# RMSNorm factors of a hybrid decoder layer: column sums turned to rows, or a product of ones with Ln, Exp and one Newton step

## Chip, core and metric

One NeuronCore of a Trainium2 chip runs the whole kernel. The metric is device microseconds of one execution, as the median of three runs. TensorE (PE) multiplies matrices, VectorE (DVE), ScalarE (ACT) and GpSimd (POOL) work element by element, SyncE (SP) issues most of the transfers.

## What is computed

One layer for 512 prompt positions and 8 single decode steps, 520 columns in all, D_MODEL 1024. Four RMSNorms stand in it: ahead of the mixer, on the 256 memory tokens, ahead of the FFN, and at the end.

```python
def rmsnorm(x, g):
    y = xf * lax.rsqrt(jnp.mean(xf * xf, axis=-1, keepdims=True) + EPS)
    return y * g

h = rmsnorm(x, norm_mix_g)
q, k, v, u, xq, gates = split_cols(h @ w_in)
# A: sliding-window attention, B: S5 state space model, C: attention over the memory tokens
mk, mv = split(rmsnorm(mem, norm_mem_g) @ w_mem_kv)
merged = sig(gA) * P_A(A) + sig(gB) * B + sig(gC) * P_C(C)
x = x + merged @ w_out
h = rmsnorm(x, norm_ffn_g)
x = x + W_down(gelu(causal_dwconv3(h @ W_gate)) * (h @ W_up))
y = rmsnorm(x, norm_final_g)
```

## The kernel before

**Layout.** Activations are kept transposed: a block of 128 features on the partitions, 520 columns (two halves of 260) along the free axis, eight such blocks for D_MODEL. All f32 values are split in a high part in fp32r and the rest, and one block product is three matmuls (`mm3`). A weight unit is 128 x 1024: SP loads it into one of two `wraw` buffers, ACT copies the high part (`whi`), DVE subtracts the low part (`wlo`), three buffers of each (`w_split`, `load`, `begin`, `ahead`). `begin(i)` asks for the loads of i+1 and i+2, `ahead(i)` for the splits of i+1 and i+2 and the load of i+3. Products go to two PSUM tiles (`mm`, `out_tile`), smaller ones to four (`SD`). Each engine works its instructions off in the order in which the program writes them.

**The norm's factor is applied late.** The products are made with x times the gain alone (`split_norm`: high part on ACT, low part on DVE). The factor rstd differs by column only, so it is multiplied in when a product is emptied from PSUM. `rstd` has 520 columns, the same on all partitions. For the mixer and the FFN, `acc` and `acc2` hold the squares summed over the eight blocks, and the sum over the partitions is still to be made.

**How rstd was made.** `rstd_cols` multiplies pieces of 88 columns of the sums, as weights, with one column of ones, so that each piece's sums stand on 88 partitions: six products for 520 columns, three for the memory's 256. DVE makes 1/sqrt on these few numbers: a bit trick and three Newton steps, twelve small operations, then a diagonal matrix of them. `rstd_rows` multiplies ones with the diagonal pieces, which puts each number on all partitions again, and ACT copies the rows out.

```python
dcol = rstd_cols([acc], (0, 1), NH)     # mixer: after the first block of q0 (Q_COL)
ahead(iq)
rstd_rows(dcol, rstd)                   # mixer: eleven blocks later (Q_ROW)
ps = product(i, range(8), blk(yh, yl), kouter=True, mid=norm2)                            # FFN: fg0
pu = product(i, range(8), blk(yh, yl), kouter=True, mid=lambda: rstd_rows(dcol, rstd))    # FFN: fu0
```

**Order around the mixer.** k and v are multiplied side by side as x arrives, into both `mm` tiles; then q0 into two `SD` tiles. `evac_kv` empties k and v on DVE with rstd, two multiplications each, then q0. The next unit, q1, writes k's tile. `x_norm` then makes the fully normalised x (DVE, ACT, DVE per block) beside q1 to q3, for the u, xq and gate units that follow.

**A planner orders the rest.** Softmax of the window attention, the memory's norm (`mem_prep`), S5 and memory attention are generators ("lanes"). `pump` runs their next steps between block products, when a clock model of all engines (`Clock`) says that the step's operands are ready; `drain` runs a lane to its end. So an instruction's place in the streams depends on the modelled times of all before it. `mem_prep` ends with the two norm steps, and `mem_kv` drains it ahead of the first memory product.

**Order around the FFN.** The out units write x1, its squares go to `acc2`. fg0 and fu0 run with all eight blocks in turn, both halves; the norm's two parts stand in the middle of the one and the other. Then DVE empties fg0 with rstd, and a lane does the convolution (`conv`: POOL, ACT, DVE twice, POOL, Gelu on ACT) and a second multiplication by rstd, after which DVE empties fu0. The next pairs fg1, fu1 use the same two tiles. Beside them a lane builds the combinations of normalised x for a Strassen product (`y_lane`).

**Activation tables.** Exp, Tanh, Gelu and Ln need a table on ACT; the loads are instructions on its queue. The kernel asks for one by name near the end, for the final norm, which uses Ln, Exp and a Newton step (`Piece.ln_exp`, `Piece.newton`).

Of the kernel before, what the change touches and what calls it, by code (L numbers as in the profile page):

```python
# [15 lines left out]
P = 128  # L16
# [270 lines left out]
N_RAW = 2  # L287
N_T2 = 11
Q_COL = (0, 0)
Q_ROW = (1, 2)  # L290
N_SWA = 2
N_MEM = 3

# [1 line left out]
def body(ctx, tc, I, O):  # L295
# [20 lines left out]
    def B(dt=F32):  # L316
        live["B"] += 1
        assert live["B"] <= 8, "no slot left"
        return big.tile([P, KB * NT], dt, name="B", tag="B")
# [12 lines left out]
    def free(*ts):  # L332
        for t in ts:
            clk.pinned.discard(t.name)
# [9 lines left out]
    def T2(n=NT, dt=F32):  # L344
        t = make(tmp, [P, 528], dt, "T2", N_T2)
        return t[:, :n]

    def TN(n):
        t = clk.tile(tny.tile([P, 8], F32, name="TN", tag="TN"), "TN", 16)
        return t[:, :n]  # L350

    def SD():
        return make(psd, [P, 512], F32, "SD", 4)
# [137 lines left out]
    def product(i, js, xs, kouter=False, mid=None):  # L491

        ps = out_tile()
        n = len(js)
        ev[0] = EV_FF if clk.late else EV if n == 8 else EVH
        if kouter:
            for k, j in enumerate(js):
                wh, wl = hl(i, j)
                for h in range(H):
                    xh, xl = xs(k, h)  # L500
                    mm3(ps[:, h, :NH], wh, wl, xh, xl, k == 0, k == n - 1)
                if k == n // 2:
                    ahead(i)
                    if mid:
                        mid()
            pump()
        else:
            for h in range(H):
                for k, j in enumerate(js):
                    wh, wl = hl(i, j)  # L510
                    xh, xl = xs(k, h)
                    mm3(ps[:, h, :NH], wh, wl, xh, xl, k == 0, k == n - 1)
                    if k % GRAIN == GRAIN - 1 and (h == 0 or k < n - 1):
                        if h == 0 and k >= 3:
                            ahead(i)
                        pump(0.325 * ((1 - h) * n + n - 1 - k))
        return ps[:, :, :NH]
# [10 lines left out]
    eps = con.tile([P, 1], F32, name="eps")  # L528
    dve.memset(eps, EPS)
    warm = con.tile([P, 1], F32, name="warm")  # L530
    act.activation(warm, ones[:, 0:1], AF.Exp)
    xraw = B()

    def x_load(k, n):
# [29 lines left out]

    RB = 88

    def starts(n):
        return (0, (n - RB) // 2, n - RB)

    def rstd_cols(parts, halves, n):  # L570

        ps = SD()
        nb = 3 * len(halves)
        for a, h in enumerate(halves):
            for b, s in enumerate(starts(n)):
                c = 3 * a + b
                for e, x in enumerate(parts):
                    pe.matmul(ps[:RB, c:c + 1], x[:, h * n + s:h * n + s + RB], ones[:, 0:1], start=e == 0,
                              stop=e == len(parts) - 1)
        v, y, t = TN(nb)[:RB], TN(nb)[:RB], TN(nb)[:RB]  # L580
        it = tny.tile([P, 16], I32, name="it", tag="it", bufs=2)[:RB, :nb]
        dve.tensor_scalar(v, ps[:RB, :nb], 1.0 / DM, EPS, op0=OP.mult, op1=OP.add)
        dve.tensor_scalar(it, v.bitcast(I32), 1, None, op0=OP.logical_shift_right)
        dve.tensor_scalar(it, it, -1.0, 1597463007.0, op0=OP.mult, op1=OP.add)
        free(ps)
        y0 = it.bitcast(F32)
        for n_ in range(3):
            dve.tensor_tensor(t, y0, y0, op=OP.mult)
            dve.scalar_tensor_tensor(t, t, -0.5, v, op0=OP.mult, op1=OP.mult)
            dve.scalar_tensor_tensor(y, t, 1.5, y0, op0=OP.add, op1=OP.mult)  # L590
            y0 = y
        d = T2(528)[:RB, :nb * RB].rearrange("p (b c) -> p b c", b=nb)
        dve.tensor_tensor(d, ident[:RB, None, :RB].to_broadcast([RB, nb, RB]),
                          y[:, :, None].to_broadcast([RB, nb, RB]), op=OP.mult)
        return d

    def rstd_row(d, a, n, ps):

        for b, s in enumerate(starts(n)):
            pe.matmul(ps[:, s:s + RB], ones[:RB, :], d[:, 3 * a + b, :], start=True, stop=True)  # L600

    def rstd_rows(d, out, n=NH, halves=(0, 1)):
        for a, h in enumerate(halves):
            ps = SD()
            rstd_row(d, a, n, ps)
            act.activation(out[:, h * n:(h + 1) * n], ps[:, :n], AF.Copy)
            free(ps)


    sv = con.tile([P, 528], F32, name="sv")  # L610
# [156 lines left out]
    sp.dma_start(mraw, I["memT"])  # L767
    iq = begin("q")
    psq = [SD(), SD()]
    dcol = None  # L770
    for h in range(H):
        for k in range(KB):
            wh, wl = hl(iq, k)
            xh, xl = xg(k, h)
            mm3(psq[h][:, :NH], wh, wl, xh, xl, k == 0, k == KB - 1)
            if (h, k) == Q_COL:
                dcol = rstd_cols([acc], (0, 1), NH)
                ahead(iq)
            if (h, k) == Q_ROW:
                rstd_rows(dcol, rstd)  # L780

    ud = drm.tile([8, 4, P, 64], F32, name="ud")
    us = drm.tile([4, P, 8], F32, name="us")
# [20 lines left out]
    def mem_prep():  # L804
        macc = T2(256)
        for k in range(KB):
            split_norm(mraw, C_GMEM, mgh, mgl, k, 256)
            sq = macc if k == 0 else T2(256)
            act.activation(sq, mraw[:, k * 256:(k + 1) * 256], AF.Square)
            if k:  # L810
                dve.tensor_tensor(macc, macc, sq, op=OP.add)
                free(sq)
            yield 1 if k == KB - 1 else "dve", 1
        d = rstd_cols([macc], (0,), 256)
        free(macc)
        yield
        rstd_rows(d, mrstd, 256, (0,))
        free(d)
        yield

    qB = B()
# [776 lines left out]
    def blk(hi, lo):  # L1598
        def f(k, h):
            o = k * NT + h * NH  # L1600
            return hi[:, o:o + NH], lo[:, o:o + NH]
        return f

    B_done(3)

    yh, yl = B(F32R), B(F32R)
    acc2 = T2()
    for m in range(8):
        i = begin("out")
# [63 lines left out]
    cpv = cpre.rearrange("p o (h b) -> p o h b", h=H)  # L1673

    def norm2():
        nonlocal dcol
        dcol = rstd_cols([acc2], (0, 1), NH)


    def conv(ob, a, c):  # L1680
# [352 lines left out]
    for ob in range(6):  # L2033
        if ob == 4:
            for name in ("A11", "S", "A12", "A22"):
                strassens[0].load(name, -1)
            cu.append(svt[:, 0:512])
            for _ in range(3):
                cu.append(hold(make(tmp, [P, 528], F32, "T2", N_T2))[:, 0:512])
            for j in range(4):  # L2040
                dparts[j][0].load(dparts[j][1])
        i = begin("fg")
        if ob == 0:

            ps = product(i, range(8), blk(yh, yl), kouter=True, mid=norm2)
            i = begin("fu")
            pu = product(i, range(8), blk(yh, yl), kouter=True, mid=lambda: rstd_rows(dcol, rstd))
            y_build = add(y_lane(), need=0, tiles=3)
            y_build.eng = "dve"
        else:  # L2050
            ps = product(i, range(8), blk(yh, yl))
        a = hold(make(tmp, [P, 528], F32, "T2", N_T2))[:, :524]
        av = wide(a)
        c = hold(T2())
        dve.tensor_tensor(av[:, :, 2:], ps, rs2, op=OP.mult)

        def first_lane(ob=ob, av=av, c=c):
            yield from conv(ob, av, c)
            yield "dve"
            dve.tensor_tensor(c, c, rstd, op=OP.mult)  # L2060

        def second_lane(ob=ob, c=c, a=a):
            act.activation(hid(ob, 0), c, AF.Copy)
            yield "dve"
            dve.tensor_tensor(hid(ob, 1), c, hid(ob, 0).bitcast(F32), op=OP.subtract)
            free(a, c)

        l = add(first_lane(), first=True, need=0)
        l.eng = "act"
        if ob:  # L2070
            i = begin("fu")
            if ob == 5:
                for s in range(D_HI):
                    cut(s, "hi")
                    if s < D:
                        cut(s, "lo")
            pu = product(i, range(8), blk(yh, yl))
        drain([l])
        dve.tensor_tensor(hv(c), pu, hv(c), op=OP.mult)
        hid_lanes[-ob] = add(second_lane(), first=True, need=0)  # L2080
        hid_lanes[-ob].eng = "act"
        while later:
            later.pop(0)[1]()

    ln = tny.tile([P, 1], F32, name="ln", tag="ln", bufs=1)
    drain([hid_lanes[-q] for q in range(6)])
    B_done(2)
    hb[1], hb[2] = B(F32R), B(F32R)
# [21 lines left out]
    class Piece:  # L2110
# [28 lines left out]
        def newton(self):  # L2139
            t = T2(self.n)  # L2140
            dve.tensor_tensor(t, self.y, self.y, op=OP.mult)
            dve.scalar_tensor_tensor(t, t, -0.5, self.v, op0=OP.mult, op1=OP.mult)
            dve.scalar_tensor_tensor(self.y, t, 1.5, self.y, op0=OP.add, op1=OP.mult)
# [195 lines left out]
```

## Time and profile before

| | |
|---|---|
| median of 3 runs | 869.74 us (869.24 to 870.06) |
| profiled execution | 870.38 us, span 868.6 us |
| PE busy | 851.2 us (98%) |
| DVE busy | 599.8 us (69%) |
| ACT busy | 409.0 us (47%) |
| POOL busy | 135.7 us (16%) |
| mean granted clock of TensorE | 0.997 |

The span is from the first to the last instruction. The profiled execution is 1.78 us longer than its span. Busy times of PE count each matmul to its modelled end, so that neighbours overlap; what a matmul costs in a running stream is read from the distance of two starts. The source column reads L259 for nearly all, a helper's line, so that stages are told by tile names and times.

### The profile page before, as it was taken

What the parts mean: (1) busy time and instruction counts of PE and PEld (TensorE: products, weight loads), DVE (VectorE), ACT (ScalarE), POOL (GpSimd) and SP (SyncE); (2) the same over time, 40 slices, a digit from 0 to 9 for tenths busy, and PEclk for the clock granted to TensorE, in tenths of its full rate; (3) what the DMA queues carried; (4) which work ended last, traced back from release to release, by engine and by line L of the source; (5) the groups of instructions that cost most, each with busy time, mean ns of one, the idle gap of its engine ahead of it and who ended that gap; (6) DMA issues with size and microseconds to landing.
All of it is one profiled execution on the core that took longest, in us unless ns stands there. A gap on an engine that the chain in (4) does not pass through costs nothing.

```text
span 868.6 us, 17715 instructions
## 1 busy us (share of the span) xinstructions
PE 851.2 (98%) x7067; PEld 823.0 (95%) x7067; DVE 599.8 (69%) x1101; ACT 409.0 (47%) x800; POOL 135.7 (16%) x370
## 2 busy tenths in 40 slices
PE   8999999999999999999999999999999999999996
PEld 8998899999789899989999999999999999999995
DVE  6786787985447698213765568787777877777756
ACT  7366565544434322223334434444645545464555
POOL 7888030000000000000000010111112110110100
PEclk9999999999999999999999999999999999999998
DMA  7534482253714523624333323557565655653222
GB/s 264 178 78 122 125 196 80 74 154 116 150 49 146 170 74 97 148 69 184 106 101 97 98 73 100 144 155 185 152 160 151 165 130 153 161 150 83 71 74 98
DMA packets 54737, 110.41 MB, mean 127 GB/s; under 512 B 13968, under 2 KB 25664, under 8 KB 54384
## 3 DMA queue, kind: packets, MB, share of 16 engines
q1 hardware_dynamic: 50816, 97.40, 38.0%
q0 software_dynamic: 3408, 11.27, 6.8%
q8 instruction: 55, 0.90, 0.4%
q10 hardware_dynamic: 432, 0.63, 0.2%
q14 instruction: 26, 0.21, 0.1%
HBM read 104.05 MB, written 6.26 MB: 127 GB/s over the span
## 4 chain that ended last, share of the span: by engine, by line
PE 74%; DVE 11%; issue 9%; ACT 3%; DMA 2%; SPq 0%; POOL 0%; DVEq 0%; ACTq 0%; POOLq 0%
PE mm L259 55%; PE SD L259 19%; DVE T L259 5%; DVE B L259 3%; DVE wlo L259 2%; DMA wraw<-in_w 2%; ACT T L259 1%; ACT whi L259 1%; ACT B L259 1%; DVE TN L259 1%; SPq L259 0%; POOL T L259 0%; DVE M L259 0%; DVEq L2334 0%; DVE it L259 0%
## 5 line engine op out<-in xcount | busy, mean ns | idle before, releaser
L259 PE MATMUL mm<-B,whi 128*128 128x260 f32 (+1 forms) x3632 | 666.5, 284 | 3.5 <-DVE B L259 1.4
L259 PEld LDWEIGHTS mm<-B,whi 128*128 128x128 f32 x3632 | 560.3, 188 | 11.9 <-issue 5.0
L259 PE MATMUL mm<-B,wlo 128*128 128x260 f32 (+1 forms) x1816 | 512.8, 282 | 1.9 <-DVE wlo L259 1.9
L259 PEld LDWEIGHTS mm<-B,wlo 128*128 128x128 f32 x1816 | 342.2, 188 | 2.8 <-DVE wlo L259 2.8
L259 DVE TENSOR_TENSOR wlo<-wraw,whi 128x1024 fp32r<-128x1024 f32 (+1 forms) x149 | 152.4, 1029 | 89.2 <-ACT whi L259 86.2
L259 ACT ACTIVATE whi<-wraw 128x1024 fp32r<-128x1024 f32 (+1 forms) x149 | 132.5, 897 | 73.0 <-PE mm L259 32.6
L259 PE MATMUL SD<-B,whi 128*128 128x260 f32 x464 | 85.9, 282 | 0.0
L259 PEld LDWEIGHTS SD<-B,whi 128*128 128x128 f32 x464 | 71.6, 188 | 0.1
L259 ACT ACTIVATE T<-mm 128x260 f32<-128x260 f32 (+3 forms) x76 | 32.5, 449 | 78.1 <-PE mm L259 78.0
L259 PE MATMUL SD<-B,wlo 128*128 128x260 f32 x232 | 65.6, 283 | 0.0
L259 ACT ACTIVATE B<-T 128x520 fp32r<-128x520 f32 (+2 forms) x48 | 29.7, 618 | 55.5 <-DVE T L259 55.4
L259 ACT ACTIVATE whi<-M 128x512 fp32r<-128x512 f32 x64 | 39.1, 624 | 26.3 <-DVE M L259 19.4
L259 DVE TENSOR_TENSOR wlo<-M,whi 128x512 fp32r<-128x512 f32 x64 | 42.8, 686 | 11.9 <-ACT whi L259 11.8
L259 DVE TENSOR_TENSOR B<-B 128x256 f32<-128x256 f32 (+11 forms) x78 | 36.3, 474 | 15.9 <-ACT B L259 14.4
L259 PEld LDWEIGHTS SD<-B,wlo 128*128 128x128 f32 x232 | 43.6, 188 | 0.0
L259 DVE TENSOR_TENSOR B<-mm,B 128x520 f32<-128x520 f32 (+2 forms) x36 | 22.4, 622 | 27.4 <-PE mm L259 26.8
L259 ACT ACTIVATE B<-SD 128x256 fp32r<-128x256 f32 (+5 forms) x44 | 17.9, 429 | 44.3 <-PE SD L259 44.3
L259 DVE TENSOR_TENSOR B<-SD,B 128x256 fp32r<-128x256 f32 (+6 forms) x43 | 16.5, 396 | 30.3 <-PE SD L259 22.7
L259 PE MATMUL SD<-B 128*64 128x72 f32 (+9 forms) x412 | 37.3, 282 | 0.0
L259 DVE SCALAR_TENSOR_TENSOR T<-T,sm,T 128x512 f32<-128x512 f32 x44 | 33.1, 753 | 2.7 <-ACT T L259 2.2
L259 DVE TENSOR_TENSOR B<-T,B 128x520 fp32r<-128x520 f32 (+2 forms) x50 | 31.2, 637 | 3.7 <-ACT B L259 3.4
L259 PEld LDWEIGHTS SD<-B 128*64 128x64 f32 (+4 forms) x412 | 25.6, 146 | 8.3 <-issue 4.0
(161 smaller groups left out, 801.8 us busy)
## 6 DMA issues: line engine op xcount, KB each, us to landing
wraw<-in_w SPq DMA_DIRECT2D x96, 512.0 KB, 3.6
M<-in_w SPq DMA_DIRECT2D x48, 256.0 KB, 3.6
wraw<-in_w SPq DMA_DIRECT2D x36, 256.0 KB, 3.3
T<-in_w SPq DMA_DIRECT2D x36, 192.0 KB, 4.4
M<-in_w POOLq DMA_DIRECT2D x8, 512.0 KB, 6.6
wraw<-in_w POOLq DMA_DIRECT2D x8, 512.0 KB, 6.3
sv<-in_w SPq DMA_DIRECT2D x12, 192.0 KB, 5.5
B<-in_xT SPq DMA_DIRECT2D x1, 2080.0 KB
```

The lines of the kernel that those rows point to most:

```text
L259: return g(*a, **k)
```

## The change

Both helpers go. `rstd_sums` multiplies a matrix of ones with the sums, which gives the total on all partitions at once, and ACT makes exp(-0.5 ln(v)) from it; ACT also writes v, the mean square plus EPS. `newton` does one Newton step on full width on DVE. In the mixer all of it stands after q0's first block, with q1's split between Exp and the copies of v (`then`). In the memory's lane it is two steps. In the FFN it stands in the middle of fg0, and nothing in fu0. A table set with Ln and Exp is asked for at the start, in place of the set that Exp brought, and again ahead of the out units.

```diff
+    ln = con.tile([P, 1], F32, name="ln")
+    nc.scalar.preload_act_table_set("natural_log_exp_and_others")
-    act.activation(warm, ones[:, 0:1], AF.Exp)
+    act.activation(warm, ones[:, 0:1], AF.Ln)
...
-    def rstd_cols(parts, halves, n):
...
-    def rstd_rows(d, out, n=NH, halves=(0, 1)):
...
+    def rstd_sums(part, out, n=NH, halves=(0, 1), then=None):
+        pr = [SD() for _ in halves]
+        for p, h in zip(pr, halves):
+            pe.matmul(p[:, :n], ones, part[:, h * n:(h + 1) * n], start=True, stop=True)
+        for p, h in zip(pr, halves):
+            act.activation(out[:, h * n:(h + 1) * n], p[:, :n], AF.Ln, bias=eps, scale=1.0 / DM)
+        o = out[:, 0:len(halves) * n]
+        act.activation(o, o, AF.Exp, scale=-0.5)
+        if then:
+            then()
+        v = T2(len(halves) * n)
+        for p, h in zip(pr, halves):
+            act.activation(v[:, h * n:(h + 1) * n], p[:, :n], AF.Identity, bias=eps, scale=1.0 / DM)
+            free(p)
+        return v, o
+
+    def newton(v, o):
+        t = T2(o.shape[1])
+        dve.tensor_tensor(t, o, o, op=OP.mult)
+        dve.scalar_tensor_tensor(t, t, -0.5, v, op0=OP.mult, op1=OP.mult)
+        dve.scalar_tensor_tensor(o, t, 1.5, o, op0=OP.add, op1=OP.mult)
+        free(t, v)
...
             if (h, k) == Q_COL:
-                dcol = rstd_cols([acc], (0, 1), NH)
+                newton(*rstd_sums(acc, rstd, then=lambda: w_split(iq + 1)))
                 ahead(iq)
-            if (h, k) == Q_ROW:
-                rstd_rows(dcol, rstd)
...
-        d = rstd_cols([macc], (0,), 256)
+        v, o = rstd_sums(macc, mrstd, 256, (0,))
         free(macc)
-        yield
-        rstd_rows(d, mrstd, 256, (0,))
-        free(d)
+        yield "dve", 1
+        newton(v, o)
         yield
...
     yh, yl = B(F32R), B(F32R)
+    nc.scalar.preload_act_table_set("natural_log_exp_and_others")
+    act.activation(ln, ones[:, 0:1], AF.Ln)
     acc2 = T2()
...
     def norm2():
-        nonlocal dcol
-        dcol = rstd_cols([acc2], (0, 1), NH)
+        newton(*rstd_sums(acc2, rstd))
...
-            pu = product(i, range(8), blk(yh, yl), kouter=True, mid=lambda: rstd_rows(dcol, rstd))
+            pu = product(i, range(8), blk(yh, yl), kouter=True)
```

## Rows read from the trace of the kernel before

**Rows 1.** Page, part 1: busy us (share of the span) and instructions by engine

```profile
PE 851.2 (98%) x7067; PEld 823.0 (95%) x7067; DVE 599.8 (69%) x1101; ACT 409.0 (47%) x800; POOL 135.7 (16%) x370
```

**Rows 2.** Table by stretches: start:end and length, busy by engine, clock, DMA

```profile
core 0: us, PE busy (x) PEld busy (x) DVE busy (x) ACT busy (x) POOL busy (x), PEclk, DMA share, GB/s
45.00:160.00 115.00, 113.64 (x946) 104.25 (x945) 90.49 (x260) 73.08 (x204) 45.95 (x139) 1.00 0.45 118
520.00:582.00 62.00, 60.06 (x493) 59.09 (x491) 50.04 (x79) 28.05 (x45) 7.72 (x25) 1.00 0.48 132
```

**Rows 3.** Timeline, TensorE around q0: start us, length us, operation, out<-in, xcount

```profile
20.61 1.03 PE L259 MATMUL SD<-ones,T 128*88 128x1 f32 x12
...
21.50 0.48 PE L259 MATMUL SD<-B,whi 128*128 128x260 f32 x2
...
25.18 1.47 PE L259 MATMUL SD<-T,ones 88*128 88x88 f32 x12
...
26.44 0.48 PE L259 MATMUL SD<-B,whi 128*128 128x260 f32 x2
...
28.21 0.28 PE L259 MATMUL SD<-B,wlo 128*128 128x260 f32 x1
...
28.32 0.40 PE L259 MATMUL mm<-B,whi 128*128 128x260 f32 x2
```

**Rows 4.** Timeline, final norm: TensorE, ScalarE and VectorE

```profile
850.43 1.04 PE L259 MATMUL SD<-T,ones 128*128 128x260 f32 x4
...
851.12 0.59 PE L259 MATMUL SD<-B,whi 128*128 128x260 f32 x2
...
851.51 0.48 ACT L259 ACTIVATE T<-SD,eps 128x260 f32<-128x260 f32 x1 [1.42 <-PE SD L259]
...
852.02 0.42 ACT L259 ACTIVATE T<-T 128x260 f32<-128x260 f32 x1
...
853.01 0.89 DVE L259 SCALAR_TENSOR_TENSOR T<-T,T 128x260 f32<-128x260 f32 x2
```

**Rows 5.** Timeline, ScalarE and VectorE around q0; idle before, and releaser, in brackets

```profile
24.31 1.06 ACT L259 ACTIVATE whi<-wraw 128x1024 fp32r<-128x1024 f32 x1 [3.62 <-PE SD L259]
...
24.72 2.35 DVE L259 TENSOR_TENSOR wlo<-wraw,whi 128x1024 fp32r<-128x1024 f32 x2
...
27.11 1.43 DVE L259 TENSOR_TENSOR B<-mm,rstd 128x512 f32<-128x512 f32 x4
...
29.25 0.75 DVE L259 SCALAR_TENSOR_TENSOR T<-B,sm,rstd 128x520 f32<-128x520 f32 x1
```

**Rows 6.** Timeline, TensorE and VectorE around the FFN's norm

```profile
499.44 1.03 PE L259 MATMUL SD<-ones,T 128*88 128x1 f32 x12
...
506.15 1.47 PE L259 MATMUL SD<-T,ones 88*128 88x88 f32 x12
...
515.47 0.48 PE L259 MATMUL mm<-B,whi 128*128 128x260 f32 x2
...
508.07 0.70 DVE L259 TENSOR_TENSOR T<-mm,rstd 128x520 f32<-128x520 f32 x1 [3.02 <-ACT rstd L259]
...
514.63 0.70 DVE L259 TENSOR_TENSOR T<-mm,T 128x520 f32<-128x520 f32 x1
```

**Rows 7.** Timeline, TensorE around the memory's norm

```profile
68.98 0.56 PE L259 MATMUL SD<-ones,T 128*88 128x1 f32 x6
...
69.40 0.49 PE L259 MATMUL mm<-B,whi 128*128 128x260 f32 x2
...
75.13 0.87 PE L259 MATMUL SD<-T,ones 88*128 88x88 f32 x6 [1.17 <-DVE TN L259]
...
75.84 0.60 PE L259 MATMUL SD<-cs,T 128*128 128x128 f32 x4
```

**Rows 8.** Timeline, ScalarE: a first gate, the first FFN scaling, a table load

```profile
158.18 0.60 ACT L259 ACTIVATE B<-mm 128x520 f32<-128x520 f32 x1 [1.43 <-PE mm L259]
...
456.68 0.73 ACT L259 ACTIVATE B<-B,sm 128x520 fp32r<-128x520 f32 x1 [2.62 <-DVE B L259]
...
833.12 1.28 ACT L2102 ACT_TABLE_LOAD   x1
...
834.42 0.20 ACT L259 ACTIVATE ln<-ones 128x1 f32<-128x1 f32 x1
```

More of the change, by code (lines that the diff above doesn't have):

```diff
@@ L289 @@
 Q_COL = (0, 0)
-Q_ROW = (1, 2)
 N_SWA = 2
@@ L565, in body @@
     RB = 88
-    def starts(n):
-        return (0, (n - RB) // 2, n - RB)
-    def rstd_cols(parts, halves, n):
[L572 to L595, printed above, removed]
@@ L597, in rstd_row @@
-    def rstd_row(d, a, n, ps):
-        for b, s in enumerate(starts(n)):
-            pe.matmul(ps[:, s:s + RB], ones[:RB, :], d[:, 3 * a + b, :], start=True, stop=True)
-    def rstd_rows(d, out, n=NH, halves=(0, 1)):
[L603 to L607, printed above, removed]
+    def rstd_sums(part, out, n=NH, halves=(0, 1), then=None):
[13 more added lines that the diff above has]
+        return v, o
@@ L769, in body @@
     psq = [SD(), SD()]
-    dcol = None
     for h in range(H):
@@ L2083, in body @@
             later.pop(0)[1]()
-    ln = tny.tile([P, 1], F32, name="ln", tag="ln", bufs=1)
     drain([hid_lanes[-q] for q in range(6)])
```

## The prediction

> **What bounds the kernel now.** I read the busy shares of the page first, to see which engine has no room: TensorE is busy 98% of the span [rows 1], so the end moves only by work that TensorE no longer does, or by stretches in which it stands. Next the table by stretches, to see where it stands: 1.36 us between 45 and 160 us, and 1.94 us between 520 and 582 us [rows 2]. Then the timeline of single engines around the three places that the change touches: TensorE for the price of the old and new products, VectorE (DVE) and ScalarE (ACT) for who delivers the norm's factor, and whether TensorE is there first. The granted clock is 1.00 in both stretches [rows 2], so durations can be added as they stand.
>
> **Mixer, TensorE's work.** In the running stream a product of 260 columns follows the last by 0.11 to 0.12 us [rows 3]. The first old group starts at 20.61 and the stream goes on at 21.50: 0.89 us. The second starts at 25.18 and the stream goes on at 26.44: 1.26 us. Removed are 2.15 us. The new product, ones by 260 columns in f32, is already in the kernel at its end: two of them hold the stream from 850.43 to 851.12, so 0.69 us [rows 4]. The mixer needs two: 2.15 - 0.69 = 1.46 us saved. The square sums are ready where the old columns start, as the old group starts without a wait [rows 3], and the new products stand at the same place.
>
> **Mixer, the new wait.** The first q product after q0 writes the bank that k's product holds, and that is emptied by two DVE multiplications with rstd. Before, DVE did them from 27.11 (two of the four in that row, half of 1.43 us), free at about 27.85; TensorE came at 28.32 [rows 3, 5]. After, TensorE comes at 28.32 - 1.46 = 26.86. DVE's chain: the first new product is done some 0.74 us after 20.61 (the final norm's two are read 1.08 us after their start, and one is 0.35 less [rows 4]), so Ln starts at 21.35. Two Ln, 0.48 each and overlapping by 0.1: 22.2. Exp on 520 columns: 0.64, between the 0.42 for 260 and the 1.06 for 1024 [rows 4, 5]: 22.9. Now `then` puts q1's split in front of the rest: its high part on ACT, 1.06, ends at 23.9, and its low part stands on DVE ahead of the Newton step, half of 2.35 [rows 5]: 25.05. Newton, three dependent operations on 520 columns: 0.70 [rows 6], 0.75 twice [rows 5], with 0.05 between them as dependent ones don't overlap (0.89 for two of 260 [rows 4]): 27.3. `ahead` then puts q2's low part in front of the evacuation, another 1.17: 28.45; its weights were split at 24.31 before [rows 5] and stand on ACT behind the two Identity, so they are in time. Two multiplications: 29.2. TensorE restarts at 29.25, 0.93 us later than before: the 1.46 us are spent and a wait of 2.4 us comes. Behind the waiting product stand all of q1 to q3 and the u products. Bounds: +0.5 if each of eight steps overlaps by 0.05 more, +1.6 if the DVE chain, which is 28.45 - 27.11 = 1.34 late, also reaches the last normalised blocks of x before u0. I take +0.93, as TensorE is late by as much itself.
>
> **Memory.** Removed: 68.98 to 69.40, 0.42 us, and 75.13 to 75.84, 0.71 us [rows 7]; added one product of 256 columns, half of 0.69. Saved: 0.78 us. The second old group also stood 1.17 us for the DVE chain [rows 7]. After the change nothing of this norm follows on TensorE; three DVE operations on 256 columns remain, some 1.35 us (0.89 for two, and a third), and are wanted only when the first memory product is emptied, some 2.7 us later. Next on TensorE are transposes of an earlier softmax step and a product whose weights were split two units ahead. Gone are 0.78 + 1.17 = 1.95 us; bounds 0.78 (another late step takes the place) and 1.95.
>
> **FFN.** The same two groups, 1.03 and 1.47 [rows 6], go and two products come: 1.46 us. Before, the rows stood in the middle of fu0, and DVE idled 3.02 us up to 508.07 to empty fg0. After, sums at 499.44 give Exp at 501.7 by the chain above and Newton at 504.1 behind fg1's split; fu1's split (fg0 ends near 502.3, then 1.06 + 1.17) puts the first multiplication at 505.2, 2.9 us earlier. TensorE then needs fu0's bank for fu1 at 515.47 - 1.46 = 514.0. It is freed by the multiplication that started 6.56 us after 508.07 and lasts 0.70 [rows 6]; with the table load of Gelu, 1.28 [rows 8], that is 505.2 + 6.56 + 1.28 + 0.70 = 513.7. Just no wait, with 0.3 us of cover: if the cover is gone, it costs up to 0.5 us. Bounds for the stage: -1.0, and -3.4 if the 2.9 us that DVE gains also close the 1.94 us of [rows 2].
>
> **Table loads.** A load lasts 1.28 us [rows 8]. The one at the start is there before, with another set. The one ahead of the out products lies in ACT's idle time there (2.62 us ahead of the first scaling [rows 8]): nothing. If Tanh is not in the set with Ln, which no row shows, the first gate brings one more; ACT idles 1.43 us ahead of that Tanh [rows 8], so it is hidden too, and would cost up to 1.28 us of ACT in a stretch where TensorE is fed two products ahead. Gelu's is counted above.
>
> [rows 8] show a load that ends at 834.40 and the next operation at 834.42: no pause behind it. The Trainium skill, ScalarE: Activation LUTs, section What ACT_TABLE_LOAD costs, gives a switch about 2.66 us, a load of about 1283 ns and a drain of about 1380 ns. The 1283 ns agree, the drain isn't seen here. By that rule of the Trainium skill Gelu would come 1.38 us later and the sum would be some 1.3 us higher.
>
> **Sum.** +0.93 - 1.95 - 1.46 = -2.48 us. The profiled execution took 870.38 (span 868.6 and 1.78 around it), so 867.9; it lies 0.64 above the median of 869.74, which gives 867.26, say 867.3, 0.28% less. A measurement of this kernel can tell about 0.2%, 1.74 us: faster means below 868.0.
>
> **The rivals.**
> *More is freed.* DVE is done 2.9 us earlier at FFN's start, and the gaps of 520 to 582 are waits for DVE. For it: DVE is busy 50.0 of 62 us there [rows 2]. Against: DVE's order is fixed by the planner, not by who is ready. 867.3 - 1.94 = 865.3.
> *Only part stays.* Another late step takes the place of the memory norm's 1.17, and 0.3 of the mixer's DVE delay reaches u0: 867.3 + 1.5 = 868.8, no difference. For it: this stretch is fed by softmax steps on DVE and ACT, and the planner, whose clock now sees other durations, orders them anew.
> *DVE's backlog is handed on.* The evacuation is 1.34 late; if x's normalised blocks, the memory product and the last attention block are each handed to TensorE 1.34 late, with TensorE there in time, the sum is 0.93 - 0.78 - 1.46 + 4.0 = +2.7: 872.4. It decides from the third such hand-over on; one only cancels the gain. For it: DVE is busy 90.5 of 115 us between 45 and 160 [rows 2]. Against: TensorE itself is 0.93 late, which leaves 0.4 of each.
> *A pause behind the load.* If ACT stands behind Gelu's load as long again, 1.28 us, fu0's bank is late by 1.0: 868.3. [rows 8] speak against it at the one place where an operation follows at once. It is the drain of the Trainium skill's page named above.
>
> **How the numbers follow.** Forecast 0.50, more freed 0.15, only part 0.24, backlog 0.09, pause 0.02. The forecast's own bounds (+0.5 to +1.3 in the mixer, FFN -1.0 to -2.0) put a fifth of it above 868.0, and a fifth of "only part" falls below. Faster: 0.40 + 0.15 + 0.05 = 0.60. Slower: 0.09. Within 0.2%: 0.31. The range of 865.0 to 869.8 holds the forecast, "more freed", "only part" and the pause with some 0.3 to 1 us around each; the backlog and the tails, under 0.2, lie outside.
>
> **What would show it.** TensorE waits about 2.4 us for DVE near 27 us and restarts near 29.25. No wait of TensorE remains ahead of the first memory product near 75. Two more products of ones stand near 499.5 with no rows behind, and DVE empties fg0 near 505, not 508 (less the shift). Loads: one ahead of the out products, one ahead of the first fold's Gelu. I am wrong if TensorE's busy time falls by less than 3.5 us (the work alone is 1.46 + 0.78 + 1.46 = 3.7), or if the stretch from 30 to 240 us has more gaps than before.

## The result, and the profile after

| | before | after |
|---|---|---|
| median | 869.74 us | 879.10 us (876.03 to 882.13, 6 runs) |
| ratio | | 1.0108, 95% interval 1.0090 to 1.0125 |
| profiled execution, span | 870.38, 868.6 | 880.5, 878.7 |
| mean granted clock of TensorE | 0.997 | 0.989 |

The changed kernel is 9.4 us slower; forecast were 2.4 us less. The page, part 1, of the changed kernel:

```profile
PE 854.1 (97%) x7017; PEld 824.5 (94%) x7017; DVE 595.9 (68%) x1071; ACT 417.1 (47%) x812; POOL 137.3 (16%) x370
```

TensorE's busy time rose by 2.9 us against [rows 1], though its work became less. The table by stretches says why (columns as in [rows 2]):

```profile
core 0: us, PE busy (x) PEld busy (x) DVE busy (x) ACT busy (x) POOL busy (x), PEclk, DMA share, GB/s
20.00:45.00 25.00, 22.83 (x175) 22.54 (x174) 17.08 (x26) 9.79 (x16) 20.73 (x54) 0.93 0.50 151
45.00:160.00 115.00, 112.89 (x927) 103.22 (x927) 86.27 (x245) 73.34 (x205) 46.22 (x138) 1.00 0.44 116
160.00:240.00 80.00, 77.67 (x637) 72.56 (x636) 55.71 (x92) 36.56 (x70) 2.48 (x5) 0.98 0.47 129
520.00:582.00 62.00, 59.67 (x491) 58.74 (x490) 44.57 (x66) 24.72 (x38) 10.33 (x26) 1.00 0.47 133
582.00:600.00 18.00, 14.14 (x98) 13.64 (x97) 15.45 (x31) 8.61 (x17) 1.54 (x3) 0.81 0.39 112
```

In three of the stretches the granted clock is below 1.00, and a matmul takes longer there. Between 582 and 600 us TensorE also stands for 3.9 us. DVE did 5.5 us less between 520 and 582 than in [rows 2] (4.7 less in a window moved by the 4 us that this kernel is late there), so that work was left for later. What TensorE waited for, in the whole span:

```profile
engine line waited for: us in total, times, longest us
PE mm L259 <- ACT B L259: 4.2, 2, 3.1
PE mm L259 <- DVE B L259: 4.2, 5, 2.2
PE SD L259 <- ACT T L259: 3.0, 2, 1.9
```

TensorE in the mixer (timeline; start us, length us, operation, tiles):

```profile
20.63 1.04 PE L259 MATMUL SD<-T,ones 128*128 128x260 f32 x4
21.32 0.59 PE L259 MATMUL SD<-B,whi 128*128 128x260 f32 x2
...
26.78 0.28 PE L259 MATMUL SD<-B,wlo 128*128 128x260 f32 x1
29.23 0.48 PE L259 MATMUL mm<-B,whi 128*128 128x260 f32 x2 [2.17 <-DVE B L259]
...
30.64 0.42 PE L259 MATMUL mm<-B,wlo 128*128 128x260 f32 x1
30.86 0.64 PE L259 MATMUL mm<-B,whi 128*128 128x260 f32 x2
31.29 0.42 PE L259 MATMUL mm<-B,wlo 128*128 128x260 f32 x1
```

The two products of ones hold the stream for 0.69 us, the wait is 2.17, and q1 starts at 29.23. Then comes what the prediction lacks: three products take 0.65 us (30.64 to 31.29) where they took 0.36 ahead of the wait. The granted clock is 0.50 between 30.0 and 32.5, which is 1.2 GHz instead of 2.4. ScalarE and VectorE on the way to that restart:

```profile
22.77 1.04 ACT L259 ACTIVATE whi<-wraw 128x1024 fp32r<-128x1024 f32 x1
...
23.84 1.26 DVE L259 TENSOR_TENSOR wlo<-wraw,whi 128x1024 fp32r<-128x1024 f32 x1 [3.12 <-ACT whi L259]
25.02 0.68 DVE L259 TENSOR_TENSOR T<-rstd 128x520 f32<-128x520 f32 x1
...
28.33 1.42 DVE L259 TENSOR_TENSOR B<-mm,rstd 128x512 f32<-128x512 f32 x4
```

The FFN's norm, 5.03 us later than before as a whole:

```profile
504.48 1.04 PE L259 MATMUL SD<-T,ones 128*128 128x260 f32 x4
...
510.03 0.69 DVE L259 TENSOR_TENSOR T<-mm,rstd 128x520 f32<-128x520 f32 x1
...
515.15 1.28 ACT L259 ACT_TABLE_LOAD   x1 [1.16 <-DVE T L259]
516.44 0.64 ACT L259 ACTIVATE T<-T 128x520 f32<-128x520 f32 x1
...
517.91 0.70 DVE L259 TENSOR_TENSOR T<-mm,T 128x520 f32<-128x520 f32 x1
```

And the start of the first Strassen product, with the tiles of x+y that DVE builds for it:

```profile
570.80 0.75 DVE L259 SCALAR_TENSOR_TENSOR T<-B,sm,rstd 128x520 f32<-128x520 f32 x1
572.91 0.75 DVE L259 SCALAR_TENSOR_TENSOR T<-B,sm,rstd 128x520 f32<-128x520 f32 x1
585.93 1.43 DVE L259 SCALAR_TENSOR_TENSOR T<-B,sm,rstd 128x520 f32<-128x520 f32 x2
...
586.72 0.42 ACT L259 ACTIVATE B<-T 128x260 fp32r<-128x260 f32 x1 [1.44 <-DVE T L259]
...
587.20 0.58 PE L259 MATMUL mm<-B,whi 128*128 128x260 f32 x1 [3.08 <-ACT B L259]
588.55 0.59 PE L259 MATMUL mm<-B,whi 128*128 128x260 f32 x1 [0.77 <-DVE B L259]
...
590.45 0.64 PE L259 MATMUL SD<-B,whi 128*128 128x260 f32 x2
590.89 0.42 PE L259 MATMUL SD<-B,wlo 128*128 128x260 f32 x1
```

The last of four groups starts at 585.93, when TensorE already stands; ACT waits for DVE's tile, and TensorE for ACT. From 586.2 to 593.0, so from within the stand on, the granted clock is at half again. In the kernel before, the two operations of the last group start long ahead of the products, and no product from 575 to 592 us waits longer than 0.25 us:

```profile
566.70 0.75 DVE L259 SCALAR_TENSOR_TENSOR T<-B,sm,rstd 128x520 f32<-128x520 f32 x1
568.81 0.76 DVE L259 SCALAR_TENSOR_TENSOR T<-B,sm,rstd 128x520 f32<-128x520 f32 x1
```

**Where the time went.** Both kernels have 2048 products with a low part of weights. The n-th of the one is set beside the n-th of the other, and the difference of their starts is the lateness (us, minus is earlier). Between 77 and 240 us the order of the softmax products differs, so nothing is read there. The first column is the scatter of the start alone.

| at (time before) | 16.2 | 26.8 | 32.9 | 70.8 | 77.2 | 255.8 | 497.5 | 512.4 | 574.7 | 589.5 | 858.4 |
|---|---|---|---|---|---|---|---|---|---|---|---|
| after | 0.0 | -1.4 | +2.5 | +2.8 | +1.1 | +4.6 | +5.0 | +3.6 | +4.1 | +10.2 | +10.1 |
| order of before | 0.0 | -1.4 | +2.5 | +2.4 | +0.4 | -1.2 | -1.2 | -2.6 | -2.8 | -2.8 | -2.8 |
| mixer alone | -0.3 | -1.7 | +2.2 | +2.0 | +2.0 | +0.9 | +0.9 | +1.0 | +1.0 | +1.0 | +1.0 |
| memory and FFN alone | -0.1 | -0.1 | -0.1 | -0.2 | -2.2 | -2.9 | -2.9 | -4.3 | -4.5 | -4.4 | -4.5 |
| before, new order | +0.5 | +0.5 | +0.5 | +9.4 | +8.6 | +8.8 | +9.2 | +9.2 | +10.1 | +15.5 | +15.5 |
| wait filled | 0.0 | -1.4 | +0.9 | +1.2 | -0.5 | +0.9 | +1.5 | +0.1 | +0.5 | +6.7 | +6.7 |
| FFN order of before | +0.4 | -1.1 | +1.3 | +1.7 | 0.0 | +1.3 | +1.8 | +0.4 | +0.2 | +0.2 | +0.2 |
| tiles of before | -0.2 | -1.7 | +0.7 | +1.0 | -0.7 | +2.9 | +3.3 | +1.9 | +3.6 | +3.6 | +3.6 |
| split first, order of before | -0.6 | -2.0 | -1.3 | -1.6 | -3.6 | -2.2 | -2.2 | -3.6 | -3.8 | -3.8 | -3.8 |
| the same, own place | -0.2 | -1.6 | -1.1 | -1.2 | -3.3 | -3.7 | -3.7 | -5.1 | -5.3 | -5.2 | -5.3 |

The first line has the two norms that gain, memory's 1.7 us and FFN's 1.4, and three places that lose: the mixer (3.9 from 26.8 to 32.9, where 2.4 were forecast), the softmax and S5 stretch (3.5), and the Strassen start (6.1). The other lines are the experiments.

In the softmax stretch the changed kernel waits for ACT in two places where the kernel before has no such wait, and no longer in one where that one has it. First the changed kernel's rows, then that of the kernel before:

```profile
147.74 1.08 PE L259 MATMUL SD<-T,B 128*64 128x256 f32 x6 [1.15 <-ACT T L259]
226.86 1.03 PE L259 MATMUL SD<-T,cs 32*16 32x512 f32 x2 [1.85 <-ACT T L259]
```

```profile
233.94 2.00 PE L259 MATMUL SD<-T,M 128*128 128x256 f32 x8 [1.12 <-ACT T L259]
```

That is 1.9 us more of waits. Behind the second the granted clock is half from 227.8 to 231.2, which cost about 1 us. This is an estimate: from 220 to 256 us the lateness of this kernel grows by 1.5 us, that of "FFN order of before", which has the same order and no half clock, falls by 0.9, and 1.4 of the difference is its shorter wait there (0.41 us). The remaining 0.6 of the 3.5 us was not followed.

### The profile page after: what moved, and what is told of

Read it like the earlier page. It is cut to its first block, busy times and chain, and to the rows that moved or that the text cites. A ratio compares the mean times of both kernels' runs of the same rounds, so it can differ in the third digit from the quotient of the medians.

```text
span 878.7 us, 17604 instructions
## 1 busy us (share of the span) xinstructions
PE 854.1 (97%) x7017; PEld 824.5 (94%) x7017; DVE 595.9 (68%) x1071; ACT 417.1 (47%) x812; POOL 137.3 (16%) x370
## 4 chain that ended last, share of the span: by engine, by line
PE 82%; DVE 9%; DMA 4%; ACT 3%; issue 1%; DVEq 0%; ACTq 0%
PE mm L259 64%; PE SD L259 18%; DMA wraw<-in_w 4%; DVE B L259 3%; DVE T L259 2%; DVE wlo L259 2%; ACT whi L259 2%; ACT T L259 1%; DMA sm<-in_sm 0%; ACT B L259 0%; DVE M L259 0%; DVE TN L259 0%; ACT rstd L259 0%; ACT M L259 0%; DVEq L2315 0%
## 5 line engine op out<-in xcount | busy, mean ns | idle before, releaser
L259 ACT ACTIVATE T<-mm 128x260 f32<-128x260 f32 (+3 forms) x76 | 32.5, 450 | 80.6 <-PE mm L259 80.4
L259 DVE TENSOR_TENSOR B<-mm,B 128x520 f32<-128x520 f32 (+2 forms) x36 | 22.4, 622 | 26.8 <-PE mm L259 26.2
L259 DVE TENSOR_TENSOR B<-SD,B 128x256 fp32r<-128x256 f32 (+6 forms) x43 | 16.2, 395 | 28.5 <-PE SD L259 22.1
```

Source lines behind the costliest of these rows:

```text
L259: return g(*a, **k)
```

## Experiments

Theory A: the three new norms have other costs in the planner's clock, the planner therefore runs its lanes in another order, and that order costs most of the loss, in the softmax stretch and ahead of the Strassen products. Theory B: the mixer's wait is as forecast, but TensorE's clock falls to half behind it. Rival C: the new operations and table loads themselves cost the time, in any order.

### The order held as before

```diff
+    def again():
+        calls[0] += 1
+        for i in RUNS.get(calls[0], ()):
+            run(every[i])
...
     def pump(rem=0.0):
-        while True:
...
+        again()
```

`RUNS` is a written list of the lanes that ran at each call in the kernel before. Three kernels have it: with the whole change, with the mixer's norm alone, and with the other two alone.

> The whole change, but the planner's runs of its lanes are held to the order in which it ran them in the kernel before, from a written list. Theory A (the planner's new order, the tiles of x+y built late above all, cost most of the loss): TensorE no longer stands 3.1 us ahead of the first Strassen product; what stays is +0.9 in the mixer and about +1.5 of half clock behind it, -1.7 for memory's norm and -1.4 for FFN's, so 869.0, between 867.5 and 870.5. Rival C (the new operations or table loads themselves cost it, in whatever order): 877 to 880, as the changed kernel. If A holds for the Strassen start alone and the softmax stretch loses its 2.5 us in any order: about 872.

> Only the mixer's norm is changed, with the lanes in the order of the kernel before; memory's and FFN's norms are as before. Theory B (the wait of 2.2 us ahead of q1 is followed by a granted clock of about a half for some 3 us): +0.9 for the wait and +1.5 for the clock, so 872.1, and granted clock near 0.5 around 30 to 33 us. If the clock fall comes only with something else of the changed kernel: 870.6 and a granted clock of 1.00 there. If the DVE backlog is handed on besides: 873.5 or more.

> The other part alone: memory's and FFN's norms are changed, the mixer's is as before, the lanes in the order of the kernel before. By the prediction's own terms 869.74 - 1.95 - 1.46 = 866.3; with what the trace of the changed kernel shows at these two places, -1.7 and -1.3, 866.7. Rival C (the table loads ahead of Gelu and Tanh, or DVE's later steps, take it back): 869.5 or more.

| | median us | ratio to before, 95% interval |
|---|---|---|
| whole change, order of before | 867.37 | 0.9974, 0.9965 to 0.9984 |
| mixer alone | 871.73 | 1.0024, 1.0015 to 1.0033 |
| memory and FFN alone | 866.13 | 0.9962, 0.9949 to 0.9975 |

The same operations in the old order are faster than before: 879.10 - 867.37 = 11.7 us hang on the order. C falls. The mixer's part loses and the others gain, each within 0.6 us of what was expected. Two rows of the first of these kernels: the wait, and the stretch behind it (the columns of the second are TensorE's busy time, granted clock, DMA share, GB/s).

```profile
29.22 0.48 PE L259 MATMUL mm<-B,whi 128*128 128x260 f32 x2 [2.19 <-DVE B L259]
```

```profile
30.00:32.50 2.50, 2.50 (x15) 0.58 0.43 170
```

The half clock is there with the order of before too, and with the mixer alone, so it belongs to the mixer's wait and not to the order. The whole change did 1.6 us better than expected, just outside its range: all three kernels gain 0.7 to 1.5 us between 77 and 256 us, which nobody had forecast. Part of it is a wait for ACT, 1.12 us at 233.94 in the kernel before and 0.23 at 232.79 here; the rest was not followed.

### The mixer's wait filled with work

```diff
                 ahead(iq)
+                spare = fill[0]
...
+    for _ in range(18):
+        nc.tensor.matmul(spare[:, :NH], hl(iq, 7)[0], xg(7, 1)[0], start=True, stop=True)
```

The changed kernel in its own order. Nothing is left out; the added products go to the PSUM tile that held the sums, and nobody reads them.

> The whole change in its own order, with 18 products of 260 columns more behind q0, whose results nobody reads: TensorE works through the wait of the mixer instead of standing. Theory B: the granted clock stays at 1.00 from 30 to 33 us, the first product of q1 still starts near 29.2, and the shift against the kernel before stays near +0.9 at 35 us instead of +2.5: the kernel ends some 1.5 us sooner than the changed one, 877.5. Rival (the half clock has another cause, as the load that the other engines draw): the half clock stays, and the time is 879 or more.

Median 876.79 us, ratio 1.0087 (1.0072 to 1.0102). The wait's place in the timeline, and the stretch behind it:

```profile
26.88 2.30 PE L769 MATMUL SD<-B,whi 128*128 128x260 f32 x18
29.21 0.48 PE L259 MATMUL mm<-B,whi 128*128 128x260 f32 x2
```

```profile
30.00:32.50 2.50, 2.50 (x23) 1.00 0.46 180
```

q1 starts when it did, and the clock stays at 1.00: the lateness at 32.9 us is 0.9 and not 2.5. This is what B forecast: 1.55 us of the mixer's loss in the changed kernel's profile are the half clock. One profile is thin evidence for the cause, as the next kernel shows. The stretch of half clock near 228 us is gone here too, where the changed kernel stood 1.85 us for ACT and this one 0.94.

### Which part of the order

The changed kernel with the order of before from the first FFN product on, and the kernel before in the order of the changed one:

```diff
         calls[0] += 1
+        if calls[0] < 947:
+            own(*x)
+            return
         for i in RUNS.get(calls[0], ()):
```

> The whole change; the planner orders the lanes of the attention stage itself, as in the changed kernel, and from the first FFN product on the lanes run in the order of the kernel before. It splits what the order costs. Theory A with two places (the softmax stretch of 76 to 240 us and the late tiles of x+y ahead of the Strassen products): against the kernel with the whole order of before, 867.4, the changed one is 6.0 us late at 536 us and 12.8 behind the Strassen start, so this one keeps the first share: 873.4, between 872 and 875, with no wait of 3 us ahead of the first Strassen product. If the late tiles come from the lateness of the attention stage itself and not from the order in the FFN: 877 or more.

> The kernel before, with its three old norms, but the lanes run in the order of the changed kernel. Theory A: the order alone does the harm, in whatever norms: 869.7 + 11.7 (879.1 against 867.4, the two orders of the changed kernel) = 881.4; between 878 and 883, with TensorE standing some 3 us ahead of the first Strassen product. Rival C (the order is bad only together with the new operations' load on ACT and DVE): 872 or less.

The first: 872.96 us, ratio 1.0034 (1.0017 to 1.0051). The lateness stays level from 574.7 to 589.5, so the FFN's order alone costs the 6.1 us. What is left by the medians, 872.96 - 867.37 = 5.6, is the attention stage's order and the clock. From 32.9 to 255.8 us this kernel keeps its +1.3, where the order of before goes from +2.5 to -1.2: 3.6 us, in a profile whose only half clock is in its last 4 us. The same profile shows the mixer's wait without a half clock behind it:

```profile
29.56 0.48 PE L259 MATMUL mm<-B,whi 128*128 128x260 f32 x2 [2.14 <-DVE B L259]
```

```profile
30.00:32.50 2.50, 2.50 (x23) 1.00 0.49 190
```

Its nine executions go from 869.9 to 876.4 us, the profiled one taking 870.6 with a mean clock of 0.998, the median one having 0.993 and that of 876.4 having 0.992: how often the clock falls differs from one execution to the next, and the median execution has some of it.

So the wait makes the half clock likely and not certain. Of the thirteen profiles on record five have this wait of 2.14 to 2.19 us: three show the half clock behind it (changed kernel, order of before, mixer alone), and two don't (this one, and the kernel of "The late tiles alone" below). None of the eight without the wait shows it there.

The second, the kernel before in the new order: 887.24 us, ratio 1.0201 (1.0187 to 1.0215). The order alone, without any new operation, costs 17 us, more than expected:

```profile
75.60 1.55 PE L259 MATMUL SD<-T,ones 88*128 88x88 f32 x6 [5.64 <-DVE T L259]
...
593.23 0.39 PE L259 MATMUL mm<-B,whi 128*128 128x260 f32 x1 [3.08 <-ACT B L259]
594.59 0.58 PE L259 MATMUL mm<-B,whi 128*128 128x260 f32 x1 [0.97 <-DVE B L259]
```

The Strassen start stands as in the changed kernel: the lateness grows there by 5.4 us without any new operation. The rest is not what theory A had. The old memory norm costs 8.1 us between 32.9 and 77.2 us: in the new order its row products follow its column products at once and wait 5.64 us for DVE's twelve operations, and the granted clock is half from 71.8 to 82.1 us. The softmax stretch, with TensorE 8.6 us late already, costs only 0.3 us (77.2 to 255.8). That 881.4 + 5.6 = 887.0 comes near the time is therefore luck, and without the new norms the order's harm is shown at the Strassen start alone; that the softmax stretch loses by the order in any kernel is not shown.

### The late tiles alone

The changed kernel's own order, but the steps of the lane `y_lane` are put at the calls where the kernel before has them (11 is this lane, the number ahead the call).

```diff
-958: [11]
+956: [11, 11]
...
-1116: [11, 11, 11, 11, 11, 11, 11, 11, 11, 11, 11, 11]
+1116: [11, 11, 11, 11, 11]
```

> The changed kernel in its own order, with the steps of one lane alone, that which builds the tiles of x+y for the first Strassen product, put where the kernel before has them. Theory A, second place: TensorE no longer stands 3.1 and 0.8 us ahead of that product and its clock stays at 1.00 there, so 6.0 of the 12.8 us go: 879.1 - 6.0 = 873.1, between 872 and 874.5. If the tiles only come late because DVE has too much to do there in any order: 877 or more.

Median 873.97 us, ratio 1.0044 (1.0029 to 1.0058): 5.1 us less than the changed kernel. TensorE between 582 and 600 us:

```profile
582.00:600.00 18.00, 17.75 (x149) 1.00 0.61 157
```

The stand and the half clock are gone there. Near 226 us this profile still has a half clock behind a wait of 2.05 us for ACT, and none behind the mixer's wait of 2.14 us. Some of the gain is paid on the way: this kernel loses 1.7 us between 512 and 575, where the changed one loses 0.5, as its waits for DVE's T tiles are 3.6 us in the whole span against 1.0.

### The split ahead of the sums

```diff
-                newton(*rstd_sums(acc, rstd, then=lambda: w_split(iq + 1)))
+                w_split(iq + 1)
+                newton(*rstd_sums(acc, rstd))
```

Once in the order of before, once in the changed kernel's own.

> The whole change in the lanes' order of before, with one thing moved: q1's weights are split ahead of the mixer's sums and not between Exp and Identity, so that their low part on DVE stands in the 3.1 us in which DVE idles (20.7 to 23.8) and no longer ahead of the Newton step. Theory B: Newton starts at the end of Exp, 22.85, and needs the Identity at 23.6, so rstd is there at 25.1, q2's low part ends near 26.3 and the bank is free at 27.0; TensorE comes at 26.9, so the wait of 2.2 us is gone and the granted clock stays at 1.00. Gain 2.2 + 1.4: 867.4 - 3.6 = 863.8. If the clock fell for another reason: 865.2. If DVE's later steps hold TensorE anyway (backlog handed on): 866 or more.

> The changed kernel in its own order, with the same one move as the run before: q1's weights are split ahead of the mixer's sums. The order of all other instructions stays that of the changed kernel. Theories A and B together: the mixer's 2.2 + 1.4 go, as with the order of before, and the rest stays: 879.1 - 3.6 = 875.5, and up to 2 us less if the half clock near 228 us also goes, as it did with the products that filled the wait. If the mixer's wait only hides a later one: 878 or more.

In its own order: 875.77 us, ratio 1.0072 (1.0058 to 1.0086), 3.3 less than the changed kernel, as expected. Its profile has no half clock near 228 us, but one from 573.2 to 576.6, where the changed kernel's has none, so the 2 us that might have come on top did not. In the order of before: 866.49, ratio 0.9968 (0.9956 to 0.9979), where 863.8 was expected. The mixer did what it should: the wait is 0.46 us, the clock 1.00, and the lateness at 32.9 is -0.8 from the start instead of +2.5. But 2.4 us are given back between 77.2 us (-3.6) and 95 us (-1.2):

```profile
85.68 0.25 DVE L259 TENSOR_SCALAR B<-cs,B 64x64 f32<-64x64 f32 x1 [2.71 <-POOL sv L259]
...
90.64 0.47 PE L259 MATMUL mm<-B,whi 128*128 128x256 f32 x2 [2.25 <-DVE B L259]
```

A small DVE operation of the one-step attention waits for a chain of POOL, with a weight split and an evacuation queued behind it, and TensorE waits for those. Its reason is the place it writes to, which POOL's chain has used as scratch. In the kernel before the same instruction runs at 86.74 without a wait, since POOL's chain ends at 85.4 there. Here it ends at 85.7, though TensorE is 3.6 us earlier, so it is the next limit.

### The wait behind POOL

First the instruction is issued one step of its lane later, then left in its place with another place to write to:

```diff
-        dve.tensor_scalar(sd64[:64], ident[:64, :64], s[:, 128:129], None, op0=OP.mult)
         free(ps)
         yield
+        dve.tensor_scalar(sd64[:64], ident[:64, :64], s[:, 128:129], None, op0=OP.mult)
```

```diff
-    sd64 = attn[:, 3288:3352]
+    sd64 = QZ[:, 0:64]
```

> The kernel with the split first and the order of before (866.5), and one DVE instruction moved: the product with the identity in the one-sample attention, which stood 2.7 us behind a chain of POOL at 85.7 with the whole of DVE's queue behind it, is issued one step of its lane later. Theory D (this wait gave back 2.3 of the 3.6 us that the mixer's move had gained): TensorE's wait of 2.25 us near 90.6 shrinks to under 0.5, 866.5 - 1.9 = 864.6, between 863.8 and 865.5. If another chain is as late there (the loaded weights, or the wait of TensorE for the moved product itself): 866 or more.

> As the kernel with the split first (866.5), and the product with the identity stays where it was in DVE's queue, but writes to columns that the POOL chain does not use, so that it has no reason to wait for POOL. Moving it one step later had only carried the wait along: TensorE then stood 2.3 us at 93.9 for that product itself, since the split of the next weights went ahead of it. Theory D: DVE goes on at 82.9 instead of 85.7, TensorE's wait near 90.6 falls from 2.25 us to under 0.5, no wait comes at 93.9: 866.5 - 2.0 = 864.5, between 863.7 and 865.5. If the weights that come with the DMA, or ACT, are as late there: 866 or more.

The first missed: 868.86 us, ratio 0.9985 (0.9976 to 0.9994), 2.4 more than without it. The wait near 90.6 was gone, and a new one took its place:

```profile
93.57 0.24 DVE L259 TENSOR_SCALAR B<-cs,B 64x64 f32<-64x64 f32 x1
...
93.87 0.43 PE L259 MATMUL SD<-B,ones 64*128 64x64 f32 x2 [2.28 <-DVE B L259]
```

```profile
95.00:97.50 2.50, 2.50 (x14) 0.50 0.23 88
```

The moved instruction now stood behind the splits and evacuations, with a product waiting for it, and the half clock followed as in the mixer. The second removed the reason for the wait: 865.09 us, ratio 0.9947 (0.9934 to 0.9961).

```profile
83.34 0.25 DVE L259 TENSOR_SCALAR B<-cs,B 64x64 f32<-64x64 f32 x1
```

```profile
90.00:92.50 2.50, 2.50 (x22) 1.00 0.37 79
```

DVE goes on 2.3 us sooner and TensorE has no gap. This is the fastest by the medians, 4.6 us under the kernel before and 14.0 under the changed one, with the change's operations in the order of before and two places mended. Its interval overlaps with that of memory and FFN alone (866.13).

## Why the prediction was wrong, point by point

- **TensorE's work: right.** The products of ones hold the mixer's stream for 0.69 us (20.63 to 21.32), as read from [rows 4].
- **The mixer's wait: right in place and size.** TensorE restarts at 29.23; 29.25 was worked out. The wait is 2.17, forecast 2.4. The order of the DVE chain (split, Newton, next split, evacuation) was as described, and moving the first split away cut the wait to 0.46 us.
- **What follows the wait: a term was missing, the first step that failed.** "Durations can be added as they stand" rested on the clock of 1.00 in [rows 2]. That was the clock of a kernel whose TensorE, once started, never stood longer than 1.2 us. The change itself brought a stand of 2.2 us, and 1.5 us of half clock behind it in three of the five profiles with that stand. Where it came, the mixer's part is +2.5 and not +0.93.
- **Memory's norm: right.** -1.95 forecast; -1.7 in the changed kernel, -2.0 in the order of before.
- **FFN's norm: right.** -1.46 forecast, -1.40 measured in every kernel that has it. With the 5.03 us of lateness, DVE empties fg0 at 505.0 (forecast 505.2) and fu0's bank is free at 513.6 (513.7). fu1 doesn't wait.
- **Table loads: right.** A load stands ahead of the first gate (160.12), so the set with Ln has no Tanh; with the order of before the same load stands there, and the gate behind it starts at 158.56, 0.38 us later than in [rows 8], which is no more than TensorE's own lateness there (0.4), so it cost nothing. Gelu's at 515.15 was in the sum. It ends at 516.43 and the next operation starts at 516.44, so the rival of a pause behind it is out here too, like at the end of [rows 8]; the drain of 1380 ns of the Trainium skill, ScalarE: Activation LUTs, section What ACT_TABLE_LOAD costs, is again not seen. (By the prediction's own 0.3 us of cover that drain would have made the sum 1.1 us higher, not 1.3.)
- **DVE's backlog handed on: rightly put low.** From 32.9 to 70.8 us the lateness grows by 0.3 us in the changed kernel and falls by 0.1 with the mixer alone; nothing like three hand-overs of 1.34.
- **The planner: the step that failed by most.** "Only part stays" had the mechanism, that the planner orders the softmax steps anew, and priced it at one lost wait of 1.5 us for the whole. It costs 11.7 us by the medians. Some 6 of them are `y_lane` ahead of the Strassen products, shown by three kernels (FFN order of before, tiles of before, and the kernel before in the new order); this place was not looked at, because nothing of the change stands there. The rest lies in the softmax stretch (3.6 us between two profiles, without half clock in either) and in the clock. The forecast's sum took the order of everything else as given. "More freed" did not come either: DVE emptied fg0 sooner, but did less between 520 and 582 us, not more.
- **The sum.** 867.3 is what the same operations take in the old order (867.37), but this is in part luck: there +1.5 of half clock stands against -1.5 between 77 and 256 us, and the prediction had neither.
- **Its own tests caught it.** TensorE's busy time did not fall by 3.5, and the gaps between 45 and 240 us are 2.1 + 2.3 us, against 1.4 + 2.2 before (the first in [rows 2]).

Open: which of the planner's costs turns its order, and why its clock takes the late tiles to be in time. Only the orders were exchanged here, not the planner's inputs.

## What to carry to other kernels

Where a planner places work by a cost model, a change of some operations is two changes, and the second, a new order of all that follows, can be several times the first: hold the old order to learn what the operations are worth, then judge the order by itself. A new wait of TensorE costs its length and may cost two thirds as much again in clock (here 1.5 us on 2.2), so look for work that can be issued ahead of a chain of dependent steps instead of inside it. When a limit is moved, the next one is often a few hundred nanoseconds away, here a DVE instruction that waited for POOL only because of the place it wrote to.

## What the runs showed of the hardware

- **Stands of TensorE and the clock.** A full stand of 2.15 to 2.3 us in a busy stream was followed, 0.5 to 1.2 us after the restart, by some 3 us at 1.2 GHz in four profiles (2.17 in the changed kernel, 2.19, 2.15 and 2.28 in experiments), and by none in three others (2.14 twice, and 2.25 us). The price is 1.5 us in each of the four. Shorter stands were followed by half clock too (1.57, 1.85 and 2.05 us) or weren't (1.30 and 1.68), so the length of a stand alone doesn't decide. With 2.30 us of work whose results nobody reads in the mixer's place the clock stayed at 1.00 in the one profile of it. In the rows three products take 0.65 us at half clock, where full speed takes 0.36, and one kernel's executions spread from 869.9 to 876.4 us with mean clocks of 0.998 to 0.991. The Trainium skill, TensorE: Matmul & The Clock Gate, Part 1, says that the clock gate grants half or full and nothing between, and that the number of slow matmuls at a kernel's start differs from run to run. The records of granted clock agree with the first, as all are 1.00 or 0.50 (a row between, like 0.58 above, averages a stretch of both); for falls in the middle of a kernel the spread above shows what the page says of the start.
- **One instruction's place.** A DVE operation of 0.25 us, issued behind a foreign chain or behind two splits, gave 866.49 and 868.86 us, and 865.09 with a free place to write to.
